# Row dot products and a softmax: from 2 MB tiles on two queues to 4 MB halves on one queue

## The chip, the cores and the metric

The kernel runs on one core of one Trainium2 chip. The metric is the device time of one execution in microseconds (us); times of the kernel are medians of several executions. One further execution is recorded by the hardware profiler. From it come the profile page and the trace, whose clock starts at the first instruction (the "span").

## What is computed

```python
B, N, D = 8, 4096, 512          # x and y: float32, random normal
gram = np.matmul(x, y.transpose(0, 2, 1))
diag = np.diagonal(gram, axis1=1, axis2=2)      # diag[b, n] = sum over d of x[b, n, d] * y[b, n, d]
diag = diag - diag.max(axis=-1, keepdims=True)
exp = np.exp(diag)
return exp / exp.sum(axis=-1, keepdims=True)    # float32, 8 x 4096
```

Only the diagonal of the product is used. So the work is one dot product of length 512 for each of 8 x 4096 rows, and then a softmax over the 4096 values of each batch. Each input has 67.1 MB and is read once, 134.2 MB together; the output has 131 KB.

## The kernel before, in words

One row of x or y has 512 float32 values, 2 KB. A tile of x holds 1024 consecutive rows: 128 partitions with KR = 8 consecutive rows each, so 16 KB in one run per partition and 2 MB in all. A tile of y is the same. There are 32 tiles of each, 4 per batch. Tiles come from a pool with 3 buffers per name (L41), which allows three x tiles and three y tiles to be in flight or in use.

The loop over the tiles (L75 to L101) issues the load of x from SyncE's queue (SP, L79) and the load of y from ScalarE's queue (ACT, L82). Then it computes 8 dot products per partition on VectorE (DVE), one `scalar_tensor_tensor` of 512 elements for each row (L87). Each multiplies a row of x by a row of y, writes the products to a scratch tile, and sums them into one column of the persistent tile `diag_sbuf`. In the profile every such step is a pair of instructions: SCALAR_TENSOR_TENSOR, and a DVE_READ_ACCUMULATOR that delivers the sum.

After the fourth tile of a batch `softmax_batch` runs on the 32 columns of that batch:

- the maximum per partition on DVE (L52), over all partitions on GpSimd (POOL, L54), its negation on DVE (L56);
- the exponential with its sum per partition on ACT (L60), and the sum over all partitions on POOL (L66);
- the reciprocal (L68) and the scaling (L69) on DVE;
- the store of the batch's 4096 results from SP's queue (L73). A partition holds four groups of 8 results, whose places in the output are apart, so the store consists of 512 runs of 32 B.

Engines work through their own instructions in order and wait for each other by semaphores, which the framework places from the data dependencies. It also orders the instructions of each engine: the trace has the reciprocal and scaling of a batch behind the dot products of the tile after it, and loads ahead of an older batch's store. A load into a buffer waits until the dot products that read the buffer's previous tile are done. A DMA-issuing instruction that waits holds up everything behind it on its queue. On SP these are x loads behind a store, on ACT they are y loads behind the exponential of L60.

Of the kernel before, what the change touches and what calls it, by code (L numbers as in the profile page):

```python
# [1 line left out]

# [5 lines left out]


@with_exitstack
def kernel(
    ctx: ExitStack,
    tc: tile.TileContext,
    x: bass.AP,
    y: bass.AP,
    out: bass.AP,
):
    nc = tc.nc
    f32 = mybir.dt.float32  # L20

    B, N, D = x.shape
    assert y.shape == (B, N, D)
    assert out.shape == (B, N)

    P = nc.NUM_PARTITIONS
    total = B * N
    n_chunks = total // P
    cpb = N // P

    KR = 8
    n_tiles = n_chunks // KR
    tiles_per_batch = N // (P * KR)
    assert tiles_per_batch * B == n_tiles

    x_flat = x.flatten_outer_dims()
    y_flat = y.flatten_outer_dims()

    out_flat = out.flatten()

    io = ctx.enter_context(tc.tile_pool(name="io", bufs=3))  # L41
    work = ctx.enter_context(tc.tile_pool(name="work", bufs=2))
    persist = ctx.enter_context(tc.tile_pool(name="persist", bufs=1))
    sm = ctx.enter_context(tc.tile_pool(name="sm", bufs=2))

    diag_sbuf = persist.tile([P, n_chunks], f32)
    result_sbuf = persist.tile([P, n_chunks], f32)

    def softmax_batch(b):
        db = diag_sbuf[:, cpb * b : cpb * (b + 1)]  # L50
        mxp = sm.tile([P, 1], f32, tag="mxp")
        nc.vector.tensor_reduce(out=mxp, in_=db, axis=mybir.AxisListType.X, op=mybir.AluOpType.max)  # L52
        mx = sm.tile([P, 1], f32, tag="mx")
        nc.gpsimd.partition_all_reduce(out_ap=mx, in_ap=mxp, channels=P, reduce_op=bass_isa.ReduceOp.max)  # L54
        neg_mx = sm.tile([P, 1], f32, tag="nmx")
        nc.vector.tensor_single_scalar(out=neg_mx, in_=mx, scalar=-1.0, op=mybir.AluOpType.mult)  # L56

        exp_b = result_sbuf[:, cpb * b : cpb * (b + 1)]
        sump = sm.tile([P, 1], f32, tag="sump")
        nc.scalar.activation(  # L60
            out=exp_b, in_=db,
            func=mybir.ActivationFunctionType.Exp,
            bias=neg_mx, scale=1.0, accum_out=sump,
        )
        ssum = sm.tile([P, 1], f32, tag="ssum")
        nc.gpsimd.partition_all_reduce(out_ap=ssum, in_ap=sump, channels=P, reduce_op=bass_isa.ReduceOp.add)  # L66
        recip = sm.tile([P, 1], f32, tag="recip")
        nc.vector.reciprocal(out=recip, in_=ssum)  # L68
        nc.vector.tensor_single_scalar(out=exp_b, in_=exp_b, scalar=recip, op=mybir.AluOpType.mult)  # L69

        res_b = result_sbuf.rearrange("p (i kr) -> p i kr", kr=KR)[:, tiles_per_batch * b : tiles_per_batch * (b + 1), :]
        dst_b = out_flat[b * N : (b + 1) * N].rearrange("(i p kr) -> p i kr", p=P, kr=KR)
        nc.sync.dma_start(out=dst_b, in_=res_b)  # L73

    for i in range(n_tiles):  # L75
        r0 = i * P * KR
        x_tile = io.tile([P, KR, D], f32, tag="xt")
        y_tile = io.tile([P, KR, D], f32, tag="yt")
        nc.sync.dma_start(  # L79
            out=x_tile, in_=x_flat[r0 : r0 + P * KR, :].rearrange("(p k) d -> p k d", p=P)  # L80
        )
        nc.scalar.dma_start(  # L82
            out=y_tile, in_=y_flat[r0 : r0 + P * KR, :].rearrange("(p k) d -> p k d", p=P)
        )
        scratch = work.tile([P, D], f32, tag="scratch")
        for k in range(KR):
            nc.vector.scalar_tensor_tensor(  # L87
                out=scratch,
                in0=x_tile[:, k, :],
                scalar=1.0,  # L90
                in1=y_tile[:, k, :],
                op0=mybir.AluOpType.mult,
                op1=mybir.AluOpType.mult,
                accum_out=diag_sbuf[:, i * KR + k : i * KR + k + 1],
            )
        if (i + 1) % tiles_per_batch == 0:
            b = (i + 1) // tiles_per_batch - 1
            softmax_batch(b)


# [1 line left out]
_INS = ['x', 'y']  # L102
_OUTS = [((8, 4096), 'float32')]


# [23 lines left out]
```

## Time and profile before

| what | value |
|---|---|
| median of 10 executions | 333.91 us (333.31 to 334.04) |
| the profiled execution | 333.71 us |
| its span, first to last instruction | 331.9 us |
| bytes read from memory | 134.22 MB |
| VectorE busy | 183.0 us (55%), 544 instructions |
| ScalarE busy | 4.6 us |
| GpSimd busy | 6.1 us |
| loads of x, of y | 32 and 32, 2048 KB each |
| stores | 8, 16 KB each |

The profiled execution took 333.71 us, 1.8 us more than its span; this part lies around the instructions. Between the first load and the last, the page's DMA row shows the 16 DMA engines busy at nine tenths or more in each of the 40 slices but the first and the last two. VectorE is idle for stretches of several microseconds between tiles.

In the profile, "idle before" a group of instructions is the time for which its engine waited just before them, with the releaser behind the arrow. A trailing `q` (SPq, ACTq, q1, q10) stands for a queue of DMA instructions or of transfers: q1 carries what SP issued and q10 what ACT issued.

### The profile page before, as it was taken

Reading aid. Unit: us, or ns where it says so; the run is one execution under the profiler, and the core shown is the slowest. Engines: PE = TensorE matmul, PEld = TensorE weight load, DVE = VectorE, ACT = ScalarE, POOL = GpSimd, SP = SyncE. Lnnn points to the kernel's source line nnn. Section 1 sums busy time; section 2 is a strip of 40 time slices with the busy share of each in tenths; the row PEclk is TensorE's granted clock in tenths of the full one; section 3 lists DMA queues with packets and bytes.
Section 4 is the critical chain, followed back from the end, with each engine's and each line's share of the span. In section 5 each row is a group of like instructions: output and inputs, shape, how many; then the busy total and the mean of one; then the engine's idle time right before and its main releaser. Section 6 shows DMA issues by size and latency. Waiting matters only on the chain.

```text
span 331.9 us, 802 instructions
## 1 busy us (share of the span) xinstructions
DVE 183.0 (55%) x544; ACT 4.6 (1%) x17; POOL 6.1 (2%) x20
## 2 busy tenths in 40 slices
DVE  0355676543089811897038860588407973089834
ACT  0000100000000000000000000000000000000000
POOL 0000000000000000000000000000000000000000
DMA  8999999999999999999999999999999999999920
GB/s 316 434 432 428 426 425 430 426 431 422 434 428 426 428 422 434 426 421 433 423 432 428 420 430 429 434 379 429 422 437 432 418 425 430 428 395 419 428 127 2
DMA packets 13446, 134.40 MB, mean 405 GB/s; under 512 B 5248, under 2 KB 5248, under 8 KB 5248
## 3 DMA queue, kind: packets, MB, share of 16 engines
q1 hardware_dynamic: 8832, 67.24, 48.8%
q10 hardware_dynamic: 4608, 67.11, 47.3%
q14 instruction: 6, 0.05, 0.0%
HBM read 134.22 MB, written 0.13 MB: 405 GB/s over the span
## 4 chain that ended last, share of the span: by engine, by line
DMA 69%; DVE 25%; issue 2%; SPq 1%; POOL 1%; ACTq 0%; POOLq 0%; DVEq 0%
DMA x_tile<-in_x_dram 53%; DVE scratch L87 24%; DMA y_tile<-in_y_dram 16%; SPq L73 1%; POOL mx L54 1%; DVE result_sbuf L69 1%; DVE mxp L52 0%; ACTq L82 0%; DVE recip L68 0%; POOLq L124 0%; DVE neg_mx L56 0%; DVEq L69 0%; POOLq L54 0%; SPq L79 0%; DVEq L87 0%
## 5 line engine op out<-in xcount | busy, mean ns | idle before, releaser
L87 DVE SCALAR_TENSOR_TENSOR scratch<-x_tile,y_tile 128x512 f32<-128x512 f32 x256 | 176.9, 691 | 139.9 <-DMA x_tile<-in_x_dram 88.2
L87 DVE DVE_READ_ACCUMULATOR scratch<-x_tile,y_tile 128x1 f32 x256 | 20.8, 81 | 0.0
L54 POOL PARTITION_ALL_REDUCE mx<-mxp x8 | 2.8, 352 | 316.5 <-DVE mxp L52 316.5
L60 ACT ACTIVATE result_sbuf<-diag_sbuf,neg_mx 128x32 f32<-128x32 f32 x8 | 2.6, 322 | 284.5 <-DVE neg_mx L56 284.5
L56 DVE TENSOR_SCALAR neg_mx<-mx 128x1 f32<-128x1 f32 x8 | 1.2, 154 | 4.3 <-POOL mx L54 4.3
L66 POOL PARTITION_ALL_REDUCE ssum<-sump x8 | 3.1, 385 | 5.8 <-ACT result_sbuf L60 5.8
L69 DVE TENSOR_SCALAR result_sbuf<-result_sbuf,recip 128x32 f32<-128x32 f32 x8 | 1.9, 241 | 0.8
L60 ACT ACT_TABLE_LOAD x1 | 1.3, 1283 | 39.1 <-DVE scratch L87 39.1
L68 DVE RECIPROCAL recip<-ssum 128x1 f32<-128x1 f32 x8 | 1.3, 158 | 1.0 <-POOL ssum L66 1.0
L52 DVE TENSOR_REDUCE mxp<-diag_sbuf 128x1 f32<-128x32 f32 x8 | 1.5, 186 | 0.3
L60 ACT ACTIVATION_READ_ACCUMULATOR result_sbuf<-diag_sbuf,neg_mx 128x1 f32 x8 | 1.5, 186 | 0.0
L113 POOL MEMSET const-float32-0.0<- 128x1 f32 x1 | 0.1, 99 | 0.2 <-issue 0.2
L113 POOL MEMSET const-bfloat16-1.0<- 128x1 bf16 x1 | 0.1, 102 | 0.0
L113 POOL MEMSET const-uint8-127<- 128x1 uint8 x1 | 0.1, 102 | 0.0
L113 POOL MEMSET const-float32-1.0<- 128x1 f32 x1 | 0.1, 100 | 0.0
## 6 DMA issues: line engine op xcount, KB each, us to landing
x_tile<-in_x_dram SPq DMA_DIRECT2D x32, 2048.0 KB, 23.5
y_tile<-in_y_dram ACTq DMA_DIRECT2D x32, 2048.0 KB, 13.7
out_dram<-result_sbuf SPq DMA_DIRECT2D x8, 16.0 KB, 17.1
```

The lines of the kernel that those rows point to most:

```text
L52: nc.vector.tensor_reduce(out=mxp, in_=db, axis=mybir.AxisListType.X, op=mybir.AluOpType.max)
L54: nc.gpsimd.partition_all_reduce(out_ap=mx, in_ap=mxp, channels=P, reduce_op=bass_isa.ReduceOp.max)
L56: nc.vector.tensor_single_scalar(out=neg_mx, in_=mx, scalar=-1.0, op=mybir.AluOpType.mult)
L60: nc.scalar.activation(out=exp_b, in_=db, func=mybir.ActivationFunctionType.Exp, bias=neg_mx, scale=1.0, accum_out=sump,)
L66: nc.gpsimd.partition_all_reduce(out_ap=ssum, in_ap=sump, channels=P, reduce_op=bass_isa.ReduceOp.add)
L68: nc.vector.reciprocal(out=recip, in_=ssum)
L69: nc.vector.tensor_single_scalar(out=exp_b, in_=exp_b, scalar=recip, op=mybir.AluOpType.mult)
L73: nc.sync.dma_start(out=dst_b, in_=res_b)
L87: nc.vector.scalar_tensor_tensor(out=scratch, in0=x_tile[:, k, :], scalar=1.0, in1=y_tile[:, k, :], op0=mybir.AluOpType.mult, op1=mybir.Al ...
L113: nc = _bacc.Bacc("TRN2", target_bir_lowering=False, num_devices=1)
```

## The change

- The rows are dealt out anew. Each partition gets R = 32 consecutive rows of a batch, so all that it handles of a batch is one run of 64 KB in x and in y. A batch is loaded in two halves of H = 16 rows: a tile has 4 MB, with a run of 32 KB per partition, 64 KB apart in memory.
- All loads, x and y in turn, are issued from SP's queue. There are still 3 buffers per name, of twice the size: 2 x 3 x 32 KB = 192 KB per partition.
- Of the 16 halves, the last but one is loaded in pieces of 8 and 8 rows, the last in pieces of 8, 4, 2, 1 and 1 rows.
- For the first 13 halves the dot products of a half are two VectorE instructions: `tensor_tensor` multiplies 16 rows of x by 16 rows of y in place (8192 elements per partition), and `tensor_reduce` sums each row. The last 3 halves keep one `scalar_tensor_tensor` per row, now in place and without the scratch tile.
- The softmax is the same. Its store goes from ACT's queue and has 128 runs of 128 B.

```diff
-    KR = 8
+    R = N // P
+    H = R // 2
...
+    xv = x.rearrange("b (p r) d -> b p r d", p=P)
+    yv = y.rearrange("b (p r) d -> b p r d", p=P)
+    ov = out.rearrange("b (p r) -> b p r", p=P)
     io = ctx.enter_context(tc.tile_pool(name="io", bufs=3))
-    work = ctx.enter_context(tc.tile_pool(name="work", bufs=2))
...
+    def load(b, r0, parts):
+        xt = io.tile([P, H, D], f32, tag="xt", name="xt")
+        yt = io.tile([P, H, D], f32, tag="yt", name="yt")
+        o = 0
+        for n in parts:
+            nc.sync.dma_start(out=xt[:, o : o + n, :], in_=xv[b, :, r0 + o : r0 + o + n, :])
+            nc.sync.dma_start(out=yt[:, o : o + n, :], in_=yv[b, :, r0 + o : r0 + o + n, :])
+            o += n
+        return xt, yt
...
+    def dots(b, r0, xt, yt):
+        c = b * R + r0
+        nc.vector.tensor_tensor(out=xt, in0=xt, in1=yt, op=mybir.AluOpType.mult)
+        nc.vector.tensor_reduce(
+            out=diag[:, c : c + H], in_=xt, axis=mybir.AxisListType.X, op=mybir.AluOpType.add
         )
...
+    def dots_by_row(b, r0, xt, yt):
+        for k in range(H):
+            c = b * R + r0 + k
             nc.vector.scalar_tensor_tensor(
-                out=scratch,
-                in0=x_tile[:, k, :],
+                out=xt[:, k, :],
+                in0=xt[:, k, :],
                 scalar=1.0,
-                in1=y_tile[:, k, :],
+                in1=yt[:, k, :],
                 op0=mybir.AluOpType.mult,
                 op1=mybir.AluOpType.mult,
-                accum_out=diag_sbuf[:, i * KR + k : i * KR + k + 1],
+                accum_out=diag[:, c : c + 1],
             )
...
-        nc.sync.dma_start(out=dst_b, in_=res_b)
+        nc.scalar.dma_start(out=ov[b], in_=rb)
...
+    for b in range(B):
+        for h in range(2):
+            n = 2 * b + h
+            parts = {2 * B - 2: [8, 8], 2 * B - 1: [8, 4, 2, 1, 1]}.get(n, [H])
+            xt, yt = load(b, h * H, parts)
+            (dots_by_row if n >= 2 * B - 3 else dots)(b, h * H, xt, yt)
+        softmax(b)
```

More of the change, by code (lines that the diff above doesn't have):

```diff
@@ L22 @@
     B, N, D = x.shape
-    assert y.shape == (B, N, D)
-    assert out.shape == (B, N)
     P = nc.NUM_PARTITIONS
-    total = B * N
-    n_chunks = total // P
-    cpb = N // P
-    KR = 8
[L32 to L39, printed above, removed]
+    R = N // P
+    H = R // 2
+    xv = x.rearrange("b (p r) d -> b p r d", p=P)
+    yv = y.rearrange("b (p r) d -> b p r d", p=P)
@@ L41 @@
+    ov = out.rearrange("b (p r) -> b p r", p=P)
     io = ctx.enter_context(tc.tile_pool(name="io", bufs=3))
-    work = ctx.enter_context(tc.tile_pool(name="work", bufs=2))
     persist = ctx.enter_context(tc.tile_pool(name="persist", bufs=1))
     sm = ctx.enter_context(tc.tile_pool(name="sm", bufs=2))
[L46 to L63, printed above, removed]
-        )
[L65 to L86, printed above, removed]
+    diag = persist.tile([P, B * R], f32, name="diag")
@@ new lines @@
+    res = persist.tile([P, B * R], f32, name="res")
+    def load(b, r0, parts):
[12 more added lines that the diff above has]
+            out=diag[:, c : c + H], in_=xt, axis=mybir.AxisListType.X, op=mybir.AluOpType.add
+        )
@@ L95, with softmax @@
             )
-        if (i + 1) % tiles_per_batch == 0:
-            b = (i + 1) // tiles_per_batch - 1
-            softmax_batch(b)
+    def softmax(b):
+        db = diag[:, b * R : (b + 1) * R]
+        rb = res[:, b * R : (b + 1) * R]
+        mxp = sm.tile([P, 1], f32, tag="mxp", name="mxp")
+        nc.vector.tensor_reduce(out=mxp, in_=db, axis=mybir.AxisListType.X, op=mybir.AluOpType.max)
+        mx = sm.tile([P, 1], f32, tag="mx", name="mx")
+        nc.gpsimd.partition_all_reduce(out_ap=mx, in_ap=mxp, channels=P, reduce_op=bass_isa.ReduceOp.max)
+        nmx = sm.tile([P, 1], f32, tag="nmx", name="nmx")
+        nc.vector.tensor_single_scalar(out=nmx, in_=mx, scalar=-1.0, op=mybir.AluOpType.mult)
+        sump = sm.tile([P, 1], f32, tag="sump", name="sump")
+        nc.scalar.activation(
+            out=rb, in_=db, func=mybir.ActivationFunctionType.Exp,
+            bias=nmx, scale=1.0, accum_out=sump,
+        )
+        ssum = sm.tile([P, 1], f32, tag="ssum", name="ssum")
+        nc.gpsimd.partition_all_reduce(out_ap=ssum, in_ap=sump, channels=P, reduce_op=bass_isa.ReduceOp.add)
+        rc = sm.tile([P, 1], f32, tag="rc", name="rc")
+        nc.vector.reciprocal(out=rc, in_=ssum)
+        nc.vector.tensor_single_scalar(out=rb, in_=rb, scalar=rc, op=mybir.AluOpType.mult)
+        nc.scalar.dma_start(out=ov[b], in_=rb)
```

## The prediction

> **What bounds the kernel now.** I read the page's first two parts, then the windows, then the chain of work that ended last, then the waits.
>
> The page's slices show a transfer-bound kernel. DMA is at 9 tenths or more nearly throughout, VectorE at 55%.
>
> ```profile
> DVE 183.0 (55%) x544; ACT 4.6 (1%) x17; POOL 6.1 (2%) x20
> ...
> DMA  8999999999999999999999999999999999999920
> ...
> HBM read 134.22 MB, written 0.13 MB: 405 GB/s over the span
> ```
>
> 405 GB/s over the span is not what the stream does while it runs. The windows (start:end, length, busy times of DVE, ACT and POOL, clock, DMA share, GB/s) split the span into the fill, clean stretches, two dips and the tail:
>
> ```profile
> 0.00:2.00 2.00, 0.00 (x0) 0.00 (x0) 0.19 (x4) 1.00 0.48 115
> 2.00:4.00 2.00, 0.00 (x0) 0.00 (x0) 0.00 (x0) 1.00 0.73 279
> 4.00:30.00 26.00, 11.19 (x32) 0.00 (x0) 0.00 (x0) 1.00 1.01 431
> 72.00:80.00 8.00, 5.59 (x16) 0.00 (x0) 0.00 (x0) 1.00 1.01 427
> 92.00:100.00 8.00, 7.17 (x23) 0.41 (x2) 0.74 (x2) 1.00 1.00 426
> 216.00:220.00 4.00, 3.28 (x12) 0.41 (x2) 0.74 (x2) 1.00 1.01 348
> 296.00:300.00 4.00, 3.31 (x11) 0.41 (x2) 0.74 (x2) 1.00 0.97 340
> 317.50:318.00 0.50, 0.00 (x0) 0.00 (x0) 0.00 (x0) 1.00 0.54 229
> 318.00:321.00 3.00, 0.03 (x1) 0.00 (x0) 0.00 (x0) 1.00 0.03 14
> ```
>
> A clean stretch runs at 426 to 431 GB/s. At 216 and 296 us the stream falls to about 345. At 317.8 us it is over, while the span has 14 us to go. The end of the chain (start, length, what) shows what fills these 14 us:
>
> ```profile
> 303.97 16.97 DMA x_tile<-in_x_dram
> ...
> 320.97 0.71 DVE scratch L87 x2
> ...
> 326.10 0.71 DVE scratch L87 x2
> ...
> 326.84 0.20 DVE mxp L52
> ...
> 328.96 0.24 DVE result_sbuf L69
> ```
>
> The last x tile counts as landed at 320.94 us, 3.1 us after the stream has faded. Then come 8 rows, 320.97 to 326.84; the softmax, to 329.20; the store, to 331.9. Nothing hides these three. The waits of SP's queue show why the stream dips: x loads wait for buffers, and stores wait on the same queue in front of them.
>
> ```profile
> SPq L79 <- DVE scratch L87: 83.0, 15, 6.5
> SPq L73 <- DVE result_sbuf L69: 80.3, 8, 24.7
> SPq L79 <- DVE mxp L52: 42.6, 7, 6.2
> ```
>
> **What the Trainium skill says.** "DMA: Bandwidth & Descriptors", section "Issuing engines are not separate DMA queues", says that queues share the same 16 DMA engines, so a second issuing queue saves issue time and adds no bandwidth. The trace agrees: between 72 and 80 us all load bytes are on q10 (427 GB/s), between 92 and 100 us all are on q1 (426). Its section "Latency and other measured facts" says that copies between memory tensors lose rate when partition rows lie at large powers of two: 207 GB/s per direction at 512 KiB, where 214 is full, and 164 at 2 MiB. The pitch goes from 16 to 64 KB here; no run shows that yet. "VectorE: DVE Perf Modes", section "The perf-mode tier table", puts fp32 `tensor_tensor` and `tensor_reduce` at 1x, and its errata section gives (N+151)/0.96 ns for the fp32 `tensor_tensor`. The trace has no large one of either, but L87 with N = 512 takes 691 ns, which the formula gives exactly.
>
> **The change part by part.**
>
> *Products in two instructions.* By the formula of that page `tensor_tensor` on N = 8192 takes 8.69 us (estimate), and `tensor_reduce` at 1x about the same; L52's 128x32 reduce at 186 ns against L68's one element at 158 ns makes 0.9 ns per element, so 7.4 to 8.7 us. A half costs at most 17.4 us and its share of a softmax some 1.5 us with waits, 18.9. Its 8.39 MB need 8.39/0.429 = 19.6 us on the DMA engines. By rows it would be 16 x 0.734 = 11.7 us: VectorE becomes slower and stays hidden. If that cover fails: three buffers leave two halves, 39 us, of transfers queued when a half lands, so VectorE may run 22 us late before loads starve. The last three halves by rows would win back 3 x 7.9 us. Cost taken: 0, and 0 as long as a half stays under about 21 us.
>
> *Loads on one queue, store moved to ACT.* SP issues 42 loads (28 of 4 MB, 4 and 10 pieces); at 0.33 us each, 14 us spread over the run, is nothing. SP loses its 8 stores; what waits on SP is now a load for a buffer only, with later loads behind it. A y load waited on ACT behind the exponential; that is gone as well. ACT has 8 exponentials and 8 stores. Each store waits for the scaling (L69 before), which may stand behind up to 17 us of VectorE work; what stands behind it on ACT is the next batch's exponential, 39 us on. So both dips should go: (428-348)/428 x 4 = 0.75 us and (428-340)/428 x 4 = 0.82 us, with smaller ones at other batches.
>
> *Stores.* Runs fall from 512 to 128. In the window at 72 us, 224 such small packets took 1.6% of 16 x 8 us, 9 ns each. Seven hidden stores: 7 x 512 x 9/16 = 2.0 us of engine time before, 0.5 after. The rate in that window did not suffer, so I take 0 and keep 1.5 us of gain as the bound.
>
> *Longer runs and pitch.* The run of 32 KB saves half the per-run overhead, of which the trace gives no size. Together with the pitch the bounds are 432 GB/s (just above the best clean stretch) and, without aliasing, 426. I take 429, the middle.
>
> *Sum of the stream.* The fill stays: 2 us at 115 and 2 at 279 are 0.79 MB by 4 us. The other 133.43 MB at 429 take 311.0 us: the stream fades at 315.0 (308.9 to 313.2 us, so 312.9 to 317.2), against 317.8.
>
> *Last landing.* Before it came 3.1 us after the fade: in 318 to 321 us the trace has two last 16 KB packets and one instruction fetch (8 KB on the instruction queue). VectorE's instructions fall from 544 to 13x2 + 48x2 + 8x4 = 154, so fetches fall too. I take 1.7 us, between 1.0 and 3.1: landing at 316.7.
>
> *Rows after the last landing.* One row of x and y arrives every 0.524/0.429 = 1.22 us, and takes VectorE 0.734. Counted from the landing of the 8-row piece: 8 rows end at 5.9; the 4-row piece is there at 4.9, ends at 8.8; 2 rows at 7.3, end at 10.3; the single rows at 8.6 and 9.8, end at 11.0 and 11.7. The end is 1.95 us behind the last landing instead of 5.87, which is 3.9 less. The small pieces cost perhaps 0.1 us of rate, up to 0.6.
>
> *Softmax and store.* Same instructions: 2.36 us from 326.84 to 329.20, then 2.7 us from L73's end of wait to the end of the span. Issued from ACT, with fewer runs, the store may gain 0.2 or lose 0.2; I take 0.
>
> Sum: 316.7 + 1.95 + 0.1 + 2.36 + 2.7 = 323.8 us of span, plus the 1.8 around it = 325.6 for such a profiled execution. The median of before is 0.2 above its profiled execution: **325.8 us**.
>
> **The rivals.**
>
> *Only the tail shrinks* (12%). The dips could come from the transfers themselves, and the late last packets could stay. Then the stream ends as before and only 3.9 us go: 330.0. For it: dips recur at 39 us, like batches, and each has small ones beside it. Against: the windows at 216 and 296 follow a load issued only when the queue had run down.
>
> *The stream gets slower* (6%), my slower case. A pitch of 64 KB puts the 128 runs of a load four times as far apart; if reads collide as the skill's table has it at 512 KiB, 207/214, the 311 us become 321.5 and the time 336. It decides from 8.1/319 = 2.5%, a clean rate below 418 GB/s. Against: 64 KB is far below the pitch where the table collapses.
>
> *The pieces don't split the wait* (3%). If the rows of the last half waited for its whole tile, 16 x 0.734 = 11.7 us would follow the last landing instead of 1.95: 335.6. Against: dependencies follow regions, not tiles, in this trace: L87 writes a column of `diag_sbuf` at 297.20 while L60 reads another batch's columns at 297.31.
>
> **How the numbers follow.** The forecast has 79%, with its own range 322.8 to 329.3: the rate gives -2.1 and +2.2, the landing -0.7 and +1.4, stores and small pieces about 0.5 each way, not all at once. A range of 322.8 to 329.5 leaves out the two slower rivals and half of the first one, near 2 in 10. About 0.2% is what a measurement of this kernel can tell from no change. Slower by more: 9%, the two rivals. Within it: 2%, where the losses of rate just eat the 3.9 us. Faster: 89%.
>
> **What would show it.** Right: no window below 415 GB/s between 10 and 300 us; the stream fades near 315; one or two rows between the last landing and the maximum's reduce; halves of 17 us on VectorE with idle time before each. Wrong: a clean rate off 429, VectorE without idle time in the middle, a last landing still 3 us behind the fade, or a store from ACT that takes over 3 us.

## The result, and the profile after

| | before | changed |
|---|---|---|
| median | 333.91 us (29 runs) | 323.38 us (8 runs, 323.33 to 324.1) |
| ratio to before, 95% interval | | 0.969 (0.9682 to 0.9699) |
| profiled execution | 333.71 | 323.33 |
| its span | 331.9 | 321.0 |

The change made the kernel 3.1% faster. The forecast was 325.8 us with a range of 322.8 to 329.5: right in its sign, 2.4 us too cautious. As the experiments show, it was also partly right for a wrong reason.

The page of the changed kernel, the lines that answer to those of before:

```profile
DVE 261.4 (81%) x154; ACT 4.6 (1%) x17; POOL 6.1 (2%) x20
...
DMA  8999999999999999999999999999999999999991
...
HBM read 134.22 MB, written 0.13 MB: 418 GB/s over the span
```

VectorE works 78 us more than before, and the kernel is faster. DMA stays at nine tenths until the last slice but one.

Its windows (start:end, length, busy times of DVE, ACT and POOL, clock, DMA share, GB/s):

```profile
60.00:220.00 160.00, 144.92 (x36) 2.06 (x10) 3.33 (x9) 1.00 1.01 433
...
313.00:314.00 1.00, 0.98 (x3) 0.00 (x0) 0.00 (x0) 1.00 1.00 365
314.00:315.00 1.00, 0.96 (x4) 0.00 (x0) 0.00 (x0) 1.00 0.13 47
```

The stream runs at 433 GB/s in the middle, where the forecast had taken 429; the kernel before had 425 over the same 160 us, dips included. It fades at about 314.1 us. In its last microsecond, with runs of 2 KB, it does 365. One caution on reading these: a transfer is credited to a window as a whole, so with 32 KB runs short windows swing (the page's slices run from 392 to 457 in the middle), and only long ones compare.

The end of the chain of work (start, length, what):

```profile
305.37 10.14 DMA yt<-in_y_dram
...
315.54 0.71 DVE xt L58 x2
...
316.27 0.20 DVE mxp L72
...
318.39 0.24 DVE res L86
```

The last landing releases VectorE at 315.54; one row follows it. The two new groups of instructions and the rows that stayed (busy, mean ns of one, idle before):

```profile
L50 DVE TENSOR_TENSOR xt<-xt,yt 128x8192 f32<-128x8192 f32 x13 | 113.0, 8689 | 33.9 <-DMA yt<-in_y_dram 33.9
L51 DVE TENSOR_REDUCE diag<-xt 128x16 f32<-128x8192 f32 x13 | 112.9, 8686 | 0.4
L58 DVE SCALAR_TENSOR_TENSOR xt<-xt,yt 128x512 f32<-128x512 f32 x48 | 30.0, 687 | 9.8 <-DMA yt<-in_y_dram 9.7
```

The span's 10.9 us split by points that both traces have:

| part | before | changed | difference |
|---|---|---|---|
| start to last landing | 320.97 | 315.54 | -5.43 |
| rows after it | 5.87 | 0.73 | -5.14 |
| softmax, to the issue of the store | 2.39 | 2.40 | 0.0 |
| store, to the end of the span | 2.67 | 2.33 | -0.34 |

Around the span lie 1.8 us before and 2.3 after, so 0.5 is given back, for a reason that no run here shows. The second row is plain. The first one needed the experiments.

### The profile page after: what moved, and what is told of

It is laid out like the page before. It is cut to its first block, busy times and chain, and to the rows that moved or that the text cites. A ratio compares the mean times of both kernels' runs of the same rounds, so it can differ in the third digit from the quotient of the medians.

```text
span 321.0 us, 345 instructions
## 1 busy us (share of the span) xinstructions
DVE 261.4 (81%) x154; ACT 4.6 (1%) x17; POOL 6.1 (2%) x20
## 4 chain that ended last, share of the span: by engine, by line
DMA 63%; DVE 33%; issue 1%; SPq 1%; POOL 1%; ACT 0%; POOLq 0%; DVEq 0%
DMA yt<-in_y_dram 63%; DVE xt L50 16%; DVE diag L51 16%; SPq L43 1%; POOL mx L74 0%; POOL ssum L83 0%; DVE mxp L72 0%; DVE xt L58 0%; ACT res L78 0%; DVE rc L85 0%; POOLq L121 0%; SPq L44 0%; DVE res L86 0%; DVE nmx L76 0%; DVEq L50 0%
## 5 line engine op out<-in xcount | busy, mean ns | idle before, releaser
L50 DVE TENSOR_TENSOR xt<-xt,yt 128x8192 f32<-128x8192 f32 x13 | 113.0, 8689 | 33.9 <-DMA yt<-in_y_dram 33.9
L51 DVE TENSOR_REDUCE diag<-xt 128x16 f32<-128x8192 f32 x13 | 112.9, 8686 | 0.4
L58 DVE SCALAR_TENSOR_TENSOR xt<-xt,yt 128x512 f32<-128x512 f32 x48 | 30.0, 687 | 9.8 <-DMA yt<-in_y_dram 9.7
L85 DVE RECIPROCAL rc<-ssum 128x1 f32<-128x1 f32 x8 | 1.3, 164 | 7.7 <-POOL ssum L83 7.7
L78 ACT ACTIVATE res<-diag,nmx 128x32 f32<-128x32 f32 x8 | 2.6, 321 | 312.3 <-DVE nmx L76 312.3
L76 DVE TENSOR_SCALAR nmx<-mx 128x1 f32<-128x1 f32 x8 | 1.2, 154 | 4.3 <-POOL mx L74 4.3
L58 DVE DVE_READ_ACCUMULATOR xt<-xt,yt 128x1 f32 x48 | 3.9, 82 | 0.0
L86 DVE TENSOR_SCALAR res<-res,rc 128x32 f32<-128x32 f32 x8 | 1.9, 242 | 0.9
L72 DVE TENSOR_REDUCE mxp<-diag 128x1 f32<-128x32 f32 x8 | 1.5, 186 | 0.3
L78 ACT ACTIVATION_READ_ACCUMULATOR res<-diag,nmx 128x1 f32 x8 | 1.5, 186 | 0.0
```

Source lines behind the costliest of these rows:

```text
L50: nc.vector.tensor_tensor(out=xt, in0=xt, in1=yt, op=mybir.AluOpType.mult)
L51: nc.vector.tensor_reduce(out=diag[:, c : c + H], in_=xt, axis=mybir.AxisListType.X, op=mybir.AluOpType.add)
L58: nc.vector.scalar_tensor_tensor(out=xt[:, k, :], in0=xt[:, k, :], scalar=1.0, in1=yt[:, k, :], op0=mybir.AluOpType.mult, op1=mybir.AluOpT ...
L76: nc.vector.tensor_single_scalar(out=nmx, in_=mx, scalar=-1.0, op=mybir.AluOpType.mult)
L78: nc.scalar.activation(out=rb, in_=db, func=mybir.ActivationFunctionType.Exp, bias=nmx, scale=1.0, accum_out=sump,)
L85: nc.vector.reciprocal(out=rc, in_=ssum)
```

## The experiments

My theory at first was that the stream got faster because it no longer runs dry: loads are issued two halves ahead. The rivals were that the length of the runs, the queues, the stores or the number of instructions did it. Times are medians. The kernel before, measured beside them, had 333.84 to 334.02. Where single DMA engines are spoken of, the source is the trace's landing records: each load has 16, one for each DMA engine's share of it.

**Shorter runs.** Every half but the last is loaded in pieces of 8 rows.

```diff
-            parts = {2 * B - 2: [8, 8], 2 * B - 1: [8, 4, 2, 1, 1]}.get(n, [H])
+            parts = {2 * B - 1: [8, 4, 2, 1, 1]}.get(n, [8, 8])
```

> The changed kernel with every 4 MB half loaded as two pieces of 8 rows, so runs of 16 KB instead of 32 KB; buffers, pitch and order are kept. Theory 'queue never dry' (the stream got faster because loads are issued two halves ahead): no change, 323.4 us within 0.4. Rival 'longer runs' (each run has a fixed cost; the packet records have 1213 ns for 32 KB and 611 for 16 KB, so 9 ns a pair): 224 runs per DMA engine become 448, 2.0 us more, 325.4.

Measured: 325.24 us (325.08 to 325.47), ratio to before 0.9736 (0.9722 to 0.9749). That is 1.9 us more than the changed kernel. In the profiled executions the last landing releases VectorE at 318.18, 2.6 us later (the part around the span is 0.5 shorter here, 1.8 us). The long window of this kernel:

```profile
60.00:220.00 160.00, 142.62 (x37) 2.07 (x10) 3.67 (x10) 1.00 1.01 429
```

It reads 429 GB/s against 433, with the same buffers and order and with twice the runs. The longer runs carry part of the gain. By the landing records 14 of the 16 DMA engines have finished the last piece by 316.98 us, against 314.70 in the changed kernel: 2.3 us for 224 more runs an engine, a little more than the 2.0 us expected from the packet records. The other 0.3 lies with one engine that is later still; why there are such engines is shown below.

**y loads on ACT.**

```diff
-            nc.sync.dma_start(out=yt[:, o : o + n, :], in_=yv[b, :, r0 + o : r0 + o + n, :])
+            nc.scalar.dma_start(out=yt[:, o : o + n, :], in_=yv[b, :, r0 + o : r0 + o + n, :])
```

> The changed kernel with the y loads issued from ACT's queue (where the stores are too), the x loads from SP's. Theory 'queue never dry': 323.4 within 0.5, since two halves stay queued whichever queue they are on. Rival 'one queue is what helps': the y loads wait behind stores and the exponential again, the dips come back, 325 or more.

Measured: 328.53 us, ratio 0.9833 (0.9819 to 0.9847), 5.2 us slower than the changed kernel. It looks like the rival's win, and it isn't. The stream is as fast: 432 GB/s from 60 to 220 us, and by the landing records the last piece lands at 315.5, as in the changed kernel. VectorE is what is late. Its timeline (start, length, engine, line, operation):

```profile
42.13 8.69 DVE L50 TENSOR_TENSOR xt<-xt,yt 128x8192 f32<-128x8192 f32 x1 [2.02 <-DMA yt<-in_y_dram]
61.63 8.69 DVE L50 TENSOR_TENSOR xt<-xt,yt 128x8192 f32<-128x8192 f32 x1 [10.81 <-DMA yt<-in_y_dram]
70.24 17.27 DVE L51 TENSOR_REDUCE diag<-xt 128x16 f32<-128x8192 f32 x2
...
87.52 8.68 DVE L50 TENSOR_TENSOR xt<-xt,yt 128x8192 f32<-128x8192 f32 x1
```

The framework ordered VectorE's instructions otherwise here: two multiplications, then their two sums. The second multiplication waits 10.81 us for its loads while the first half's sum, ready to run, stands behind it. Time lost like this was not won back here: the rows of the last half run without a pause until after 320 us. The rival's price came true by another mechanism. On the queues themselves this experiment says that the rate does not depend on one or two.

The same kernel shows one more cost. The all-partition maximum beside a multiplication, on POOL:

```profile
87.70 8.71 POOL L74 PARTITION_ALL_REDUCE mx<-mxp  x1 [87.27 <-DVE mxp L72]
```

Alone it takes 0.35 us. Here it lasts as long as the multiplication of 8.68 us that began just before it. The Trainium skill, "SBUF — State Buffer", section "SBUF: two separate sides", says that VectorE operations with two inputs in SBUF and a GpSimd operation that reads SBUF take turns at a shared port pair, the later one being blocked for a whole instruction. These numbers agree.

**No pieces.** The last two halves are loaded whole.

```diff
-            parts = {2 * B - 2: [8, 8], 2 * B - 1: [8, 4, 2, 1, 1]}.get(n, [H])
+            parts = [H]
```

> The changed kernel with the last two halves loaded whole. The last landing is then followed by 16 rows at the 0.613 us step seen in the changed kernel, 9.8 us, instead of one row at 0.73: 9.1 more, less the 0.5 to 0.9 us that the short runs of the small pieces cost the stream: 331.8. Rival: the pieces are of little use because the rows waited for all of them, then no change, 323.4.

Measured: 331.66 us (331.59 to 332.14), ratio 0.9932 (0.9919 to 0.9946). The pieces are worth 8.3 us of the changed kernel. The last landing releases VectorE at 315.01 here, 0.53 us earlier than with pieces: that is the price of the short runs.

**Deeper buffers in the kernel before.**

```diff
-    io = ctx.enter_context(tc.tile_pool(name="io", bufs=3))
+    io = ctx.enter_context(tc.tile_pool(name="io", bufs=6))
```

> The kernel before with 6 buffers per name instead of 3, the same 192 KB per partition as the changed kernel; nothing else. Theory 'queue never dry': the dips at 216 and 296 us and the small ones go, the stream fades at about 315.3 instead of 317.8, and the time is 331.6. Rivals 'longer runs' or 'fewer store runs' as the cause of the faster stream: still 333.9 within 0.5.

Measured: 333.88 us (333.55 to 334.08), ratio 0.9996 (0.9987 to 1.0004): no difference. My theory fell with this run. Its windows at the places of the dips, and at the end:

```profile
216.00:220.00 4.00, 3.31 (x11) 0.41 (x2) 0.73 (x2) 1.00 1.00 426
296.00:300.00 4.00, 3.31 (x11) 0.41 (x2) 0.73 (x2) 1.00 1.01 430
...
317.00:318.00 1.00, 0.00 (x0) 0.00 (x0) 0.00 (x0) 1.00 0.08 33
...
319.00:320.00 1.00, 0.00 (x0) 0.00 (x0) 0.00 (x0) 1.00 0.06 25
```

The dips are gone, as I had expected, and the stream fades 2 us earlier. But a trickle goes on to 320 us. A DMA share of 0.06 is one engine out of 16. By the landing records, 15 engines finish the last tile by 316.9 and the 16th at 321.1, and a tile counts as landed with the last of them. In the kernel before, with the dips, the 15 engines finish only at 318.7 and the 16th at 320.95: the dips had only let this engine catch up with the others. Across the dip at 216 us its lag falls from 1.7 to 1.2 us and across the one at 296 us from 1.9 to 1.25, while with 6 buffers it stays at 2.2 and 3.2.

The second theory came from the instruction queue. The part of the page on DMA queues (packets, MB, share), asked from 20 to 312 us, in the kernel before; with 6 buffers it has the same line:

```profile
q14 instruction: 5, 0.04, 0.0%
```

And in the changed kernel:

```profile
q14 instruction: 1, 0.01, 0.0%
```

Each is a fetch of 8 KB of instructions. With 6 buffers the late engine is 3.2 us behind after these five, and 4.2 us after a sixth at 319.7, which directly follows one of that engine's last packets; the kernel before has a sixth at 319.5. In the changed kernel the lag is 0.8 us after its one fetch. That makes some 0.6 to 0.8 us a fetch. The Trainium skill, "Runtime: NRT & Kernel Launch", section "Instruction fetch mechanics", says that each engine's sequencer fetches its next block of instructions over a DMA queue of its own while the current block runs, at a cost that is mostly hidden, in blocks of 16 KiB. Here the packets have 8 KB, and the theory was that next to a saturated load stream the cost isn't hidden. The next run tests it.

**One instruction per row everywhere in the changed kernel**, so 544 VectorE instructions instead of 154:

```diff
-            (dots_by_row if n >= 2 * B - 3 else dots)(b, h * H, xt, yt)
+            dots_by_row(b, h * H, xt, yt)
```

> The changed kernel with one instruction per row in all 16 halves: VectorE gets less busy, its instructions rise from 154 to 544. Theory 'instruction fetches': a fetch of 8 KB falls on one of the 16 DMA engines and sets its loads back by about 0.83 us (the gap between the 15th and the 16th engine's landing steps up by that when the changed kernel's one fetch occurs, and a tile counts as landed with the slowest engine), so some four more fetches give 3.3 us more, 326.7, with the fade of the other 15 engines unchanged. Rival 'the two-instruction form is neutral' (step of the prediction: cost 0): 323.4 within 0.4.

Measured: 326.48 us (326.32 to 326.51), ratio 0.9776 (0.9763 to 0.979), 3.1 us slower with 62 us less of VectorE work between 60 and 220 us. Its fetches from 20 to 312 us, and then its windows at the end:

```profile
q14 instruction: 4, 0.03, 0.0%
```

```profile
314.00:315.00 1.00, 1.00 (x3) 0.00 (x0) 0.00 (x0) 1.00 0.17 64
...
316.00:317.00 1.00, 1.00 (x4) 0.00 (x0) 0.00 (x0) 1.00 0.06 25
317.00:318.00 1.00, 0.71 (x4) 0.00 (x0) 0.00 (x0) 1.00 0.05 18
```

15 engines fade at the same time as in the changed kernel, and one goes on for three microseconds more. The landing records show the fetches one by one: the lag of the last engine behind the 15th goes from 0.5 to 1.4 us with the fetch at 125 us, to 2.4 with the one at 185 and to 3.4 with the one at 263. The last landing releases VectorE at 318.22, 2.7 us later, for three more fetches: 0.9 each. The other 0.8 of its span lies in its last store, for which no cause is shown.

**Fewer instructions in the kernel before**, with 6 buffers:

```diff
+        if i < n_tiles - 2:
+            nc.vector.tensor_tensor(out=x_tile, in0=x_tile, in1=y_tile, op=mybir.AluOpType.mult)
+            nc.vector.tensor_reduce(
+                out=diag_sbuf[:, i * KR : (i + 1) * KR], in_=x_tile,
+                axis=mybir.AxisListType.X, op=mybir.AluOpType.add,
+            )
...
-        for k in range(KR):
+        for k in range(KR if i >= n_tiles - 2 else 0):
```

> The kernel before with 6 buffers per name and, for all tiles but the last two, the products of a tile in one instruction and their sums in another, so fewer VectorE instructions; loads, runs of 16 KB, two queues and the 8-row tail stay. Theory 'instruction fetches': with the queue never dry and the late engine gone, the last tile lands some 3.3 us earlier: 330.6. Rival, the late engine has another cause: 333.9 within 0.5, as with 6 buffers alone.

Measured: 342.78 us, ratio 1.0267 (1.0253 to 1.0281). The expected time was missed by 12 us, and yet the landing went as expected. The windows:

```profile
316.00:317.00 1.00, 1.00 (x2) 0.00 (x0) 0.81 (x1) 1.00 0.29 44
317.00:318.00 1.00, 1.00 (x1) 0.00 (x0) 1.00 (x1) 1.00 0.00 0
```

No trickle: the last tile lands at 317.4 by the landing records, 3.7 us before that of the run with 6 buffers alone. This kernel has two instruction fetches before its last landing instead of six. Neither of the two left an engine late at the end (0.15 us behind the 15th); why is open. The rest of the 340.6 us of span is VectorE, late as in the run with two queues. The chain of this kernel:

```profile
316.19 4.38 POOL mx L54
...
321.38 4.33 DVE diag_sbuf L87
...
326.45 7.43 DVE scratch L93 x24
```

A tile's sum stands behind a negation that waits for the all-partition maximum, and that waits for a multiplication: 4.38 us instead of 0.35. In two instructions VectorE has little slack, and an order that waits for others spends it.

**More instructions on an idle engine**: 336 one-element copies on ACT in the changed kernel.

```diff
+    spare = persist.tile([P, 48], f32, name="spare")
...
+            for j in range(48 if n % 2 == 0 and n < 2 * B - 3 else 0):
+                nc.scalar.activation(
+                    out=spare[:, j : j + 1], in_=diag[:, b * R + j % H : b * R + j % H + 1],
+                    func=mybir.ActivationFunctionType.Copy, scale=1.0,
+                )
         softmax(b)
```

> The changed kernel with 48 one-element copies on ACT after the first half of each of the first seven batches (336 more instructions, into a spare tile that nothing reads); ACT is idle then, and VectorE's instructions and all loads are as they were. Theory 'instruction fetches': at some 125 instructions a fetch, as in the kernel before, two or three fetches more, 0.8 us each on the engine that they fall on: 324.2 to 325.9, with one DMA engine late at the last landing. Rival 'it is VectorE's row form that makes the last engine late': 323.4 within 0.3.

Measured: 324.42 us (324.17 to 324.56), ratio 0.9713 (0.9699 to 0.9726), 1.0 us slower, with ACT far from the critical chain. From 20 to 312 us it has 4 instruction fetches, three more, as the run with rows everywhere. They cost 1.0 us here, not 2.7. By the landing records at the end, the last engine is 1.2 us later than in the changed kernel, and the one before it 1.1 us later too. So the fetches fell on more than one DMA engine. At three of the four (83, 162 and 261.5 us) one engine falls back by 0.65 to 0.7 us each time; at the one at 242 us, which the changed kernel has as well (240.5), another falls back by 1.0. The two lags don't add up at the last landing. It is fetches that delay, not VectorE's form of work. By what rule they are dealt out to the engines stays open.

**Fewer rows in the changed kernel**: half 13 also in two instructions.

```diff
-            (dots_by_row if n >= 2 * B - 3 else dots)(b, h * H, xt, yt)
+            (dots_by_row if n >= 2 * B - 2 else dots)(b, h * H, xt, yt)
```

> The changed kernel with the 14th half (number 13) also in two instructions, so that only the last two halves go by rows: 30 VectorE instructions fewer. Theory 'instruction fetches': if this keeps the one fetch of 8 KB out of the load stream, the last landing comes 0.8 us earlier, 322.6; if the fetch stays, 323.4. VectorE ends the 14th half at about 293.5 and is through with the next 16 rows before the last half's pieces come, so nothing is added.

Measured: 323.31 us (323.12 to 323.52), ratio 0.9682 (0.9669 to 0.9695). The fetch stayed in the stream, and the time stayed too. It decides nothing between the theories.

**Rows in place in the kernel before.** The scratch tile and its pool go.

```diff
-        scratch = work.tile([P, D], f32, tag="scratch")
...
-                out=scratch,
+                out=x_tile[:, k, :],
```

> The kernel before with the products of a row written in place of the row of x instead of into the one scratch tile; nothing else. If the scratch tile is what spaces the rows at 0.734 us (each row must wait for the row before it to be through with the same buffer), the step becomes the 0.613 us of the changed kernel and the 8 rows after the last landing take 1.0 us less: 333.0. Rival, the step has another cause: 333.9 within 0.3.

Measured: 332.95 us (332.86 to 333.04), ratio 0.9971 (0.9959 to 0.9982), 0.9 us faster. Two rows of its timeline after the last landing:

```profile
321.08 0.69 DVE L85 SCALAR_TENSOR_TENSOR x_tile<-x_tile,y_tile 128x512 f32<-128x512 f32 x1 [5.56 <-DMA x_tile<-in_x_dram]
...
321.70 0.69 DVE L85 SCALAR_TENSOR_TENSOR x_tile<-x_tile,y_tile 128x512 f32<-128x512 f32 x1
```

The next row starts 0.62 us after the one before (0.613 as a mean of the 8), 0.07 us before that one's 0.69 us are over. With the scratch tile the step is 0.734: each row starts only some 0.04 us after the row before has ended. The shared buffer is the one thing that this edit took away, so it is what had kept the rows apart.

**Stores in 512 runs in the changed kernel.**

```diff
-        nc.scalar.dma_start(out=ov[b], in_=rb)
+        nc.scalar.dma_start(
+            out=out[b].rearrange("(i p k) -> p i k", p=P, k=8),
+            in_=rb.rearrange("p (i k) -> p i k", k=8),
+        )
```

> The changed kernel with its stores cut into 512 runs of 32 B as before (the results of a batch go to permuted places; nothing else is changed). If the time of small packets adds up on the DMA engines, seven hidden stores cost 7 x (32 x 9 - 8 x 13) ns = 1.3 us an engine more, and the last one 0.2: 324.9. If they hide between the loads, only the last: 323.6.

Measured: 323.82 us (323.67 to 324.02), ratio 0.9697 (0.9684 to 0.971), 0.4 more. The last landing releases VectorE at 315.54 as before, so the seven stores under the loads cost nothing. The span grows by 0.4, all of it between the issue of the last store and the end: 2.7 us instead of 2.3.

**An earlier shift, and both edits.** The reduce of the maximum moves to the first half's columns and is issued right after that half.

```diff
-        nc.vector.tensor_reduce(out=mxp, in_=db, axis=mybir.AxisListType.X, op=mybir.AluOpType.max)
+        nc.vector.tensor_reduce(
+            out=mxp, in_=diag[:, b * R : b * R + H], axis=mybir.AxisListType.X, op=mybir.AluOpType.max
+        )
...
+            if h == 0:
+                nmx = shift(b)
+        softmax(b, nmx)
```

> The changed kernel with the softmax shifted by the maximum of the first 2048 rows of a batch, known half a batch earlier, instead of that of all 4096; the quotient is the same for any shift, as long as no exponent overflows. This takes the reduce, the all-partition maximum and the negation, 316.27 to 317.20 in the changed kernel, off the end: 0.9 us less, 322.5. Rival: the wait for the last row's sum, or ACT's start, takes the place of part of it: 323.0.

Measured: 322.60 us (322.49 to 322.73), ratio 0.9659 (0.9646 to 0.9672), 0.8 less than the changed kernel. Its timeline at the end has the exponential right behind the last row:

```profile
315.65 0.69 DVE L58 SCALAR_TENSOR_TENSOR xt<-xt,yt 128x512 f32<-128x512 f32 x1 [0.50 <-DMA yt<-in_y_dram]
316.45 0.32 ACT L83 ACTIVATE res<-diag,nmx 128x32 f32<-128x32 f32 x1 [29.87 <-DVE xt L58]
```

The other edit was half 13 in two instructions, as above.

> The two edits together: the 14th half in two instructions and the shift by the first half's maximum. If each gives what is expected of it alone, 0.8 + 0.9 less than the changed kernel, 321.7; if only the shift works, 322.5.

Measured: 322.47 us (322.28 to 322.58), ratio 0.9654 (0.9641 to 0.9668). Only the shift works. Both kernels beat the changed one; between them the measurement cannot tell.

## Why the prediction was right, and where it wasn't

*Tail after the last landing: mechanism right, size too small.* The forecast took 1.95 us, on rows at a step of 0.734 us. In place the step is 0.613, so VectorE keeps up with the pieces (a row arrives every 1.22 us), and only the last row, 0.73 us, is left. The term gave 5.1 us instead of 3.9. That the products no longer share a scratch tile is in the diff, and I gave it no price. The run of the kernel before with rows in place shows it alone: 0.9 us for 8 rows.

*Small pieces: inside the bounds.* I took 0.1 and named 0.6 as the end; it was 0.53.

*Dips: the step that failed.* "So both dips should go" held, but the 0.75 and 0.82 us booked for them were worth nothing by themselves. With 6 buffers the dips go and the time stays (0.9996). I had read the rate of 16 engines together, while the end is set by the one engine that is furthest behind. Once that engine is no longer late, the others set the end, and they finished at 318.7 with the dips and at 316.9 without. So the dips may have had to go for the fetches' gain to count in full; no run here takes away the fetches and leaves the dips.

*Last landing: right direction, wrong weight.* I saw the two late packets and the fetch, and took 1.7 us behind the fade instead of 3.1; it came 1.4 behind it. I held this for a detail of the last microseconds. It is the sum of the fetches since the loads began: six before the last landing of the kernel before, one in the changed kernel. With 6 buffers, four fewer brought the landing from 321.1 to 317.4, 3.7 us.

*Longer runs: unknown cost, middle taken.* The bound of 432 GB/s was too low, since the middle of the stream reads 433. The run with 16 KB pieces puts the step at about 2.3 us. The pitch of 64 KB did no visible harm: that run has it too, and reads 429 where the kernel before has 426 to 431 in clean stretches.

For the landing's -5.43 us the experiments give -2.3 (longer runs), -3.7 (fetches, with the dips gone) and +0.5 (pieces), or -5.5. That the sum closes this well proves little: each part comes from another pair of kernels, and is good to a few tenths. The forecast had the landing 4.3 us earlier, and part of that is luck: what it booked on the dips stood in for what the fetches gave.

*Queues:* no effect on the rate, as the section of the Trainium skill says that the prediction names. *Hidden stores:* 0, as taken. *Last store:* taken at 0, gained 0.3, which the run with 512 runs explains. *Products in two instructions:* the multiplication took 8689 ns, where the estimate from the Trainium skill's formula in the prediction was 8.69 us, and the sums 8686 ns; both were hidden. The cover was thinner than I wrote, though. In two runs the loads landed as early as expected, and yet one came out 5 us slower than the changed kernel and the other 9 us slower than the kernel before, since another order of VectorE's instructions used up the slack. This order is the framework's and was not in my sum at all.

*The rivals.* "Only the tail shrinks" gave 330.0; the landing moved as well. The pieces do split the wait (8.3 us). The slower rate did not come.

## What to carry to other kernels

A load lands with the slowest of the 16 DMA engines, so a mean rate, and dips in it, can mislead: look for a trickle after the stream has faded, and ask what else that engine had to carry. Where loads fill all engines, a block of instructions costs transfer time on the engine that fetches it, so two long instructions can beat 16 short ones even though they keep VectorE busier (here by 3.1 us). Cut the last transfers fine only as far as the consumer keeps up, and check the order of the instructions before trusting a cover of a microsecond or two.

## What was not expected of the hardware

- An instruction fetch of 8 KB beside a saturated load stream set one DMA engine back by 0.65 to 1.0 us where the landing records show the step, though the packet itself takes some 0.3 us in the packet records. For the first fetch of the run with rows everywhere only 0.35 us of it showed, and for the two of the kernel before with fewer instructions nothing at the end; why is open.
- Runs of 32 KB take 1213 ns in the packet records and runs of 16 KB 611: 9 ns for each run saved. That makes 2.0 us here; 2.3 were measured at the last landing.
- The all-partition maximum of 0.35 us on POOL lasted 8.71 us beside a two-input multiplication on VectorE.
- One-row products took 0.734 us a row into one scratch tile and 0.613 us in place.
